# Moving the weight sums of a Strassen product behind its second product, and the setup's tables from GpSimd to VectorE

## The chip, the cores and the metric

The kernel runs on one core of a Trainium2 chip. The metric is the device time of one execution in microseconds, the median over the runs shown. Profiles come from one profiled execution; their times count from the start of its span.

## The reference

A decoder trunk of two layers on an input of 1024 tokens by 1024 features: an mLSTM layer (a matrix memory, worked through in chunks) and a layer of sliding-window attention with three dilations over a shared K and V. What matters here are the large projections around them, all in float32:

```python
# mLSTM layer, INNER_A = 2048, 4 heads of 512
xm, z, o_pre = jnp.split(x @ w_in, 3, axis=-1)
xc = jax.nn.silu(causal_dwconv(xm, conv_w, conv_b))
q = headwise(xc, wq)                       # blocks of 4 features, wq: 4x4 each
k = headwise(xc, wk)
v = headwise(xm, wv)
gates = jnp.concatenate([q, k, v], axis=-1) @ w_if + b_if
...
h = jax.nn.sigmoid(shp(o_pre).astype(jnp.float32)) * h_tilde
...
# shared K and V, once for three dilation groups
kv = (x @ w_kv).reshape(bsz, s, 2 * N_GROUPS_B, HEADS_B, HEAD_DIM_B)
```

The change touches the products for `o_pre` (weights in_w_o, two pairs of heads) and for the three V of the second layer (weights in_w_v, one per group), and the small tables made of wq, wk, wv and w_if at the start.

## The kernel before

A float32 product is made of three matmuls on split operands: `split` (L93, L94) casts a tile to a short float format on ScalarE (the high part, L93) and subtracts it from the tile on VectorE (the low part, L94); `mm3` (L98, L99, L100) multiplies high by high, high by low and low by high. So TensorE's L98 needs only L93, while L99 or L100 waits for L94.

The five large products with 512 columns run through `strassen_wide`. It is Strassen's scheme in Winograd's form: seven products of quarters in place of eight, with sums and differences of the weights' quarters (`sums`, L313, on VectorE, two instructions of 128x1024 for each sum) and of the results (`plus`, L317). A quarter of the weights is a pair of tiles that a DMA loads. The quarters are overwritten in place: b12 = b22 − b12, then b11 = b12 + b11, later b21 = b21 − b11 and b11 = b22 − b11. The products follow each other as b11, b21, then b11 (the new one), b12 and so on. Each `product` goes through four steps k; each step splits 128x512 of the weights into a pair of tiles (a ring of four slots in the w_o calls, s36, s37, s47, s49; of three in the w_v calls, s40, s41, s42) and issues four `mm3`, one for each of four PSUM banks.

`strassen_wide` is a generator; at each `yield` other work is put beside it: in the w_o calls the gate tables and the mLSTM's first steps, in the w_v calls the attention of the second layer. The order of each engine's instructions is not the order of the code: the program is scheduled by a simulated timeline (`schedule_with_timeline_sim=True`, L1678), which also lets `issue_after(instruction)` hold a block of instructions behind a given one. An engine runs its own list in that order, one after the other, and a wait for data holds up all that stands behind. The operands x of the second layer (the L144 and L154 differences of 128x1024 and their L93 and L94 splits) are made in the same time as the first w_v call, with the transposes L1022 and their evictions L1026 (VectorE) and L1028 (ScalarE) ahead of them.

`setup` makes the tables: `spread` (L419) puts the small blocks of wv on a 128x128 diagonal each, `through` (L426 to L428) multiplies w_if through wq, wk and wv, L457 adds two of the results, and a split makes `wprime`. The loads are in_wvT and in_wifr. All of that is on GpSimd (POOL). `setup_scores`, which the code puts in at the first `yield` of the second w_o call, uses the same two helpers. At the time of setup VectorE works for the first large product (the xm and z stream: L227, L233, L246, L250, L263, L264, L94).

Of the kernel before, what the change touches and what calls it, by code (L numbers as in the profile page):

```python
# [14 lines left out]
ALU = mybir.AluOpType  # L15
# [3 lines left out]
P = 128  # L19
# [4 lines left out]
NC_A = INNER // P  # L24
# [13 lines left out]
def f(ap):  # L38
    return ap.bitcast(F32)
# [22 lines left out]
class Kernel:  # L62
# [57 lines left out]
    def operands(self, raws, slots, engs, spare=None, s4_eng=None, fine=()):  # L120
# [3 lines left out]

        V, G = self.nc.vector, self.nc.gpsimd
        quarter = {"11": (0, 0), "12": (0, 1), "22": (1, 1), "s1": (0, 0), "s2": ("s2",) if spare else (1, 1), "s3": (1, 0), "s4": (0, 1)}
# [164 lines left out]
    def strassen_wide(self, raw, x, banks, dest, done, eng):  # L291


        V, A = self.nc.vector, self.nc.scalar
        sub, add = ALU.subtract, ALU.add
        b11, b12, b22, b21 = raw
        banks = Ring(*banks)
        new = lambda: [self.bank(i) for i in banks.next()]
        u2, u3 = [[t[:, j] for t in [self.slot(self.u_slots, (P, 2, 512)) for _ in range(2)] for j in range(2)]
                  for _ in range(2)]  # L300

        def product(acc, w, xp, first):
            for k in range(4):
                wh, wl = self.pair(self.w_hl)
                self.split(wh, wl, w[k // 2][:, k % 2 * 512:k % 2 * 512 + 512], eng)
                xh, xl = [p[k // 2][:, k % 2] for p in xp]
                for t in range(4):
                    ts = slice(t * P, t * P + P)
                    self.mm3(acc[t], xh[:, ts], xl[:, ts], wh, wl, first and k == 0, k == 3, skip=True)

        def sums(o, p, q, op):
            for j in range(2):
                eng.tensor_tensor(o[j], p[j], q[j], op=op)  # L313

        def plus(outs, ps, qs):
            for o, p, q in zip(outs, ps, qs):
                V.tensor_tensor(o, p, q, op=add)  # L317

        def result(half, i, p, q):
            o = dest(half, i)  # L320
            plus(o, p, q)
            done(half, i, o)

        a = new()
        product(a, b11, x["11"], True)
        yield
        for o, p in zip(u2, a):
            A.copy(o, p)
        sums(b12, b22, b12, sub)
        sums(b11, b12, b11, add)  # L330
        product(a, b21, x["12"], False)
        yield
        done(0, 0, a)
        b = new()
        product(b, b11, x["s2"], True)
        yield
        plus(u2, u2, b)
        c = new()
        product(c, b12, x["s3"], True)
        yield  # L340
        plus(u3, u2, c)
        sums(b21, b21, b11, sub)
        sums(b11, b22, b11, sub)
        d = new()
        product(d, b11, x["s1"], True)
        yield
        result(1, 1, u3, d)
        product(c, b21, x["22"], False)
        result(1, 0, u2, c)
        yield  # L350
        product(d, b22, x["s4"], False)
        result(0, 1, u2, d)
        yield
# [21 lines left out]
    def build(self):  # L375
        nc, tc = self.nc, self.tc
        with ExitStack() as top:
# [29 lines left out]
            self.dram["P"] = self.t(self.dp, [HA, SEQ], tag="dP")  # L407
            self.dram["G"] = self.t(self.dp, [HA, 64], tag="dG")
            self.attend = self.layer_a_attend()
# [4 lines left out]
            self.layer_b()  # L414


    def spread(self, dst, src, n):

        self.nc.gpsimd.tensor_tensor(dst.rearrange("p c (n j) -> p c n j", j=4),  # L419
                                     src.unsqueeze(2).to_broadcast([P, n, 32, 4]),  # L420
                                     self.mask.unsqueeze(1).unsqueeze(3).to_broadcast([P, n, 32, 4]), op=ALU.mult)

    def through(self, dst, w, rep, m):

        G = self.nc.gpsimd
        G.tensor_tensor(rep, rep, w.unsqueeze(3).to_broadcast([P, NC_A, 4, m]), op=ALU.mult)  # L426
        G.tensor_tensor(rep[:, :, 0:2], rep[:, :, 0:2], rep[:, :, 2:4], op=ALU.add)
        G.tensor_tensor(dst, rep[:, :, 0], rep[:, :, 1], op=ALU.add)  # L428

    def setup(self):  # L430


        nc, a, cp = self.nc, self.a, self.cp
        A, G = nc.scalar, nc.gpsimd
        self.mask = self.const("mask32", [P, 32], tag="em")
        w3 = self.slot(50, (P, 3, NC_A, 4))
        for i, n in enumerate("qkv"):
            nc.sync.dma_start(w3[:, i], a[f"w{n}T"])
        wqT, wkT, wvT = w3[:, 0], w3[:, 1], w3[:, 2]
        self.wv = []  # L440
        for i, c0 in enumerate((0, 7, 14)):
            n = (7, 7, 2)[i]
            t = self.slot(47 + i, (P, n, 136)) if i < 2 else self.t(cp, [P, n, 136], tag="k3")
            for c in range(n):
                self.wv.append(t[:, c])
            self.spread(t[:, :, 0:P], wvT[:, c0:c0 + n], n)
        g3 = self.t(cp, [P, 3, NC_A, 8], tag="k2")
        gates = []
        for i, w in enumerate((wqT, wkT, wvT)):
            rep = self.slot(51, (P, NC_A, 4, 8))  # L450
            nc.sync.dma_start(rep, a["wifr"][i])
            g = g3[:, i]
            self.through(g, w, rep, 8)
            gates.append(g)
        for c in range(NC_A):
            A.copy(self.wv[c][:, P:P + 8], gates[2][:, c])
        G.tensor_tensor(gates[0], gates[0], gates[1], op=ALU.add)  # L457
        self.wprime = self.t(cp, [P, NC_A, 16], F32R, tag="k1")
        self.split(self.wprime[:, :, 0:8], self.wprime[:, :, 8:16], gates[0], G)

    def setup_scores(self):
        nc, a = self.nc, self.a
        t = self.slot(40)
        w, wkr, at = [t[:, lo:hi] for lo, hi in ((0, 64), (64, 320), (320, 384))]
        w, at = [v.rearrange("p (c i) -> p c i", i=4) for v in (w, at)]
        wkr = wkr.rearrange("p (c i m) -> p c i m", i=4, m=4)
        nc.sync.dma_start(w, a["wqT"])
        nc.sync.dma_start(wkr, a["wkr"])
        self.through(at, w, wkr, 4)
        for i in range(2):  # L470
            bd = self.slot(41 + i, (P, 8, P))
            self.spread(bd, at[:, 8 * i:8 * i + 8], 8)
            for j in range(2):
                cs = slice(512 * j, 512 * j + 512)
                hl = self.slot(43 + j, (P, 2, 512), F32R)
                self.split(hl[:, 0], hl[:, 1], bd.rearrange("p c m -> p (c m)")[:, cs], nc.gpsimd)
                nc.sync.dma_start(self.dram["A", i][:, :, cs], f(hl))
# [1204 lines left out]
```

## Time and profile before

| | |
|---|---|
| median of 3 runs | 2017.71 us (2016.01 to 2018.58) |
| the profiled execution | 2017.29 us, of which the span is 2015.5 us |
| mean granted clock | 0.996 |
| TensorE busy | 97% of the span |
| VectorE, ScalarE, GpSimd busy | 72%, 49%, 8% |

A row of the timeline gives the start in the span, the duration, the engine, the line, what is written and read (buffer numbers left out), the shape, and in brackets how long the engine had been idle before and what ended it. A duration on VectorE overlaps a little with that of its neighbour, so that the distance of two starts is what an instruction costs in a row of many. TensorE's matmuls of 128x512 follow each other at 0.23 us though each is shown with 0.39.

### The profile page before, as it was taken

To read this page: it belongs to the slowest core of one execution; us is meant where nothing else is said; L and a number is where in the kernel's file an instruction comes from. 1 tells how busy PE (TensorE), PEld (TensorE's weight loads), DVE (VectorE), ACT (ScalarE), POOL (GpSimd) and SP (SyncE) were. 2 spreads that over 40 slices of the span, in tenths; PEclk is the share of its full clock that TensorE was granted. 3 is DMA by queue.
4 is the path that set the end of the run, shared out by engine and by line. 5 is a ranking of instruction groups with operands and counts; after the bars stand their busy time and mean duration, and the time that the engine had idled before them with its cause. 6 is when DMAs were issued, how large, how long until landed. Compare 5 with 4: busy or idle time off the path is not lost.

```text
span 2015.5 us, 26595 instructions
## 1 busy us (share of the span) xinstructions
PE 1962.4 (97%) x9521; PEld 1626.3 (81%) x9521; DVE 1444.8 (72%) x2854; ACT 992.5 (49%) x1990; POOL 158.7 (8%) x127
## 2 busy tenths in 40 slices
PE   9999999999999999999999999999999999999997
PEld 7778888778888888878788888877887788887776
DVE  8778778675577776457867765776568887776878
ACT  5455555535645543343524542565255456676621
POOL 0200000022145343000000000000000000000000
PEclk9999999999999999999999999999999999999999
DMA  4445464456754543526121143225325622224753
GB/s 170 146 164 193 164 224 172 147 172 227 271 204 164 192 163 117 184 62 232 53 73 53 55 154 106 71 97 178 134 91 203 225 95 85 84 95 154 269 198 126
DMA packets 117916, 300.65 MB, mean 149 GB/s; under 512 B 13652, under 2 KB 31508, under 8 KB 117784
## 3 DMA queue, kind: packets, MB, share of 16 engines
q1 hardware_dynamic: 117784, 298.95, 43.2%
q8 instruction: 75, 1.23, 0.3%
q14 instruction: 57, 0.47, 0.1%
HBM read 206.32 MB, written 92.59 MB: 148 GB/s over the span
## 4 chain that ended last, share of the span: by engine, by line
PE 73%; DVE 12%; DMA 8%; ACT 4%; issue 2%; SPq 0%; POOL 0%; DVEq 0%; ACTq 0%
PE b L98 23%; PE b L100 22%; PE b L99 22%; DVE s L94 3%; DMA s<-in_w_qk 2%; PE b L603 1%; DMA s<-df 1%; ACT s L93 1%; PE b L1278 1%; DMA s<-in_w_z 1%; ACT s L1264 1%; DMA s<-in_xq 1%; PE b L609 1%; PE b L878 1%; DVE s L1415 1%
## 5 line engine op out<-in xcount | busy, mean ns | idle before, releaser
L99 PE MATMUL b<-s,s 128*128 128x512 f32 (+3 forms) x2720 | 1035.3, 382 | 9.2 <-DVE s L94 9.2
L100 PE MATMUL b<-s,s 128*128 128x512 f32 (+3 forms) x2720 | 1021.3, 382 | 4.8 <-DVE s L94 4.7
L98 PE MATMUL b<-s,s 128*128 128x512 f32 (+2 forms) x2720 | 1001.2, 386 | 20.1 <-ACT s L93 16.3
L94 DVE TENSOR_TENSOR s<-s,s 128x512 fp32r<-128x512 f32 (+2 forms) x704 | 507.5, 736 | 279.1 <-ACT s L93 273.4
L93 ACT CAST s<-s 128x512 fp32r<-128x512 f32 (+2 forms) x708 | 436.6, 636 | 541.2 <-PE b L100 308.8
L98 PEld LDWEIGHTS b<-s,s 128*128 128x128 f32 x2720 | 511.7, 188 | 124.7 <-ACT s L93 24.4
L99 PEld LDWEIGHTS b<-s,s 128*128 128x128 f32 x2720 | 512.4, 188 | 107.3 <-DVE s L94 13.2
L100 PEld LDWEIGHTS b<-s,s 128*128 128x128 f32 x2720 | 510.5, 188 | 105.5 <-DVE s L94 9.5
L233 DVE TENSOR_TENSOR s<-s,b 128x512 f32<-128x512 f32 x132 | 89.8, 681 | 27.3 <-PE b L100 25.9
L1264 ACT ACTIVATE s<-s,nmax 128x128 f32<-128x128 f32 (+1 forms) x192 | 84.3, 441 | 45.9 <-DVE nmax L1262 45.6
L94 DVE TENSOR_TENSOR s<-b,s 128x512 fp32r<-128x512 f32 (+1 forms) x96 | 51.5, 552 | 34.7 <-ACT s L93 34.3
L568 DVE SCALAR_TENSOR_TENSOR s<-s,c_convw,s 128x512 f32<-128x512 f32 (+3 forms) x96 | 71.5, 755 | 3.1 <-ACT s L565 2.6
L227 DVE TENSOR_TENSOR s<-s,b 128x512 f32<-128x512 f32 x88 | 59.5, 679 | 16.2 <-PE b L100 11.5
L317 DVE TENSOR_TENSOR s<-s,b 128x512 f32<-128x512 f32 x100 | 63.3, 680 | 8.1 <-PE b L100 7.8
L246 DVE TENSOR_TENSOR s<-s,s 128x512 f32<-128x512 f32 x44 | 30.3, 690 | 50.5 <-DMA s<-in_w_qk 23.5
L812 ACT ACTIVATE s<-s,k 128x128 f32<-128x128 f32 x144 | 47.2, 392 | 39.0 <-DVE s L94 18.5
L313 DVE TENSOR_TENSOR s<-s,s 128x1024 f32<-128x1024 f32 x40 | 49.6, 1247 | 20.8 <-DMA s<-in_w_o 11.7
L1260 DVE CUSTOM_DVE_ANT_0 s<-b,k 128x128 f32<-128x128 f32 (+1 forms) x192 | 57.2, 345 | 6.5 <-PE b L100 4.4
L93 ACT CAST s<-b 128x512 fp32r<-128x512 f32 (+1 forms) x96 | 43.8, 479 | 23.4 <-PE b L100 13.4
L771 POOL TENSOR_TENSOR s<-s 128x512 fp32r<-128x512 f32 x32 | 43.5, 1372 | 75.2 <-ACT s L770 65.5
L1211 DVE SCALAR_TENSOR_TENSOR s<-s,s 128x512 fp32r<-128x512 f32 x48 | 42.4, 885 | 9.6 <-ACT s L1210 9.1
L882 POOL TENSOR_TENSOR s<-s,s 128x512 f32<-128x512 f32 x32 | 42.3, 1337 | 65.0 <-DVE s L881 48.5
(182 smaller groups left out, 1489.0 us busy)
## 6 DMA issues: line engine op xcount, KB each, us to landing
s<-in_w_qk SPq DMA_DIRECT2D x48, 512.0 KB
s<-in_w_out SPq DMA_DIRECT2D x40, 512.0 KB
dp<-s SPq DMA_DIRECT2D x32, 512.0 KB
s<-dp SPq DMA_DIRECT2D x32, 512.0 KB
s<-in_w_v SPq DMA_DIRECT2D x24, 512.0 KB
dg<-s SPq DMA_DIRECT2D x24, 512.0 KB
s<-dg SPq DMA_DIRECT2D x24, 512.0 KB
s<-df SPq DMA_DIRECT2D x24, 512.0 KB
```

The costliest lines, as they stand in the source:

```text
L93: self.nc.scalar.copy(h, src)
L94: self.last_split = (l_eng or self.nc.vector).tensor_tensor(l, src, f(h), op=ALU.subtract)
L98: mm(ps, lh, rh, start=start, stop=False, skip_group_check=skip)
L99: mm(ps, lh, rl, start=False, stop=False, skip_group_check=skip)
L100: mm(ps, ll, rh, start=False, stop=stop, skip_group_check=skip)
L227: V.tensor_tensor(o, p, q, op=add)
L233: V.tensor_tensor(o, p[lane][rows], q[lane][rows], op=add)
L313: eng.tensor_tensor(o[j], p[j], q[j], op=op)
L317: V.tensor_tensor(o, p, q, op=add)
L568: V.scalar_tensor_tensor(u[i][:, lo:o + 512], xm[i][:, lo - s:o + 512 - s], convw[:, c, 3 - s:4 - s], u[i][:, lo:o + 512], op0=ALU.mult, o ...
L1260: V.tensor_tensor_reduce(out=dst, in0=sc, in1=bias, op0=ALU.add, op1=ALU.max, scale=1.0, scalar=-3e38, accum_out=mx[:, b:b + 1])
L1264: self.last_exp = A.activation(res[b][0], res[b][0], AF.Exp, bias=nm[:, b:b + 1], accum_out=stat[:, 1, g, b:b + 1])
```

## The change

In `strassen_wide` the sums b12 and b11 are issued after the low part of the last split of the second product. In `setup`, `spread`, `through`, the sum of gates and the low part of `wprime` are on VectorE; `setup_scores` hands in GpSimd, as before.

```diff
@@ strassen_wide
         for o, p in zip(u2, a):
             A.copy(o, p)
-        sums(b12, b22, b12, sub)
-        sums(b11, b12, b11, add)
         product(a, b21, x["12"], False)
+        with self.tc.issue_after(self.last_split.ins):
+            sums(b12, b22, b12, sub)
+            sums(b11, b12, b11, add)
         yield
@@ spread, through, setup
-    def spread(self, dst, src, n):
-        self.nc.gpsimd.tensor_tensor(...)
+    def spread(self, dst, src, n, eng):
+        eng.tensor_tensor(...)
-    def through(self, dst, w, rep, m):
-        G = self.nc.gpsimd
-        G.tensor_tensor(rep, rep, w.unsqueeze(3).to_broadcast([P, NC_A, 4, m]), op=ALU.mult)
-        G.tensor_tensor(rep[:, :, 0:2], rep[:, :, 0:2], rep[:, :, 2:4], op=ALU.add)
-        G.tensor_tensor(dst, rep[:, :, 0], rep[:, :, 1], op=ALU.add)
+    def through(self, dst, w, rep, m, eng):
+        eng.tensor_tensor(rep, rep, w.unsqueeze(3).to_broadcast([P, NC_A, 4, m]), op=ALU.mult)
+        eng.tensor_tensor(rep[:, :, 0:2], rep[:, :, 0:2], rep[:, :, 2:4], op=ALU.add)
+        eng.tensor_tensor(dst, rep[:, :, 0], rep[:, :, 1], op=ALU.add)
-            self.spread(t[:, :, 0:P], wvT[:, c0:c0 + n], n)
+            self.spread(t[:, :, 0:P], wvT[:, c0:c0 + n], n, V)
-            self.through(g, w, rep, 8)
+            self.through(g, w, rep, 8, V)
-        G.tensor_tensor(gates[0], gates[0], gates[1], op=ALU.add)
+        V.tensor_tensor(gates[0], gates[0], gates[1], op=ALU.add)
-        self.split(self.wprime[:, :, 0:8], self.wprime[:, :, 8:16], gates[0], G)
+        self.split(self.wprime[:, :, 0:8], self.wprime[:, :, 8:16], gates[0])
@@ setup_scores
-        self.through(at, w, wkr, 4)
+        self.through(at, w, wkr, 4, nc.gpsimd)
-            self.spread(bd, at[:, 8 * i:8 * i + 8], 8)
+            self.spread(bd, at[:, 8 * i:8 * i + 8], 8, nc.gpsimd)
```

Since the timeline orders the program anew, other rows move with these. Below, names carry the tile's number; a number that differs by a few between the two programs is the same tile of the text.

VectorE in the second w_o pair, before. The splits s36_648 to s47_651 are the weights of the first pair's last product (quarter b22, tiles s32_589 and s33_590); s52_661 is half of the second pair's b12.

```order
L94 TENSOR_TENSOR s36_648_3670<-s32_589_3195,s36_648_3670 128x512
L313 TENSOR_TENSOR s52_661_3774<-s35_663_3778,s52_661_3774 128x1024
L94 TENSOR_TENSOR s37_649_3685<-s32_589_3195,s37_649_3685 128x512
L317 TENSOR_TENSOR s38_646_3658<-s8_591_3199,b4_624_3450 128x512
L94 TENSOR_TENSOR s49_650_3700<-s33_590_3196,s49_650_3700 128x512
```

The same place in the changed program, and then the place where the sum stands now, behind s47_686, the last split of product 2.

```order
L94 TENSOR_TENSOR s36_648_3670<-s32_589_3195,s36_648_3670 128x512
L94 TENSOR_TENSOR s37_649_3685<-s32_589_3195,s37_649_3685 128x512
L317 TENSOR_TENSOR s38_646_3658<-s8_591_3199,b4_624_3450 128x512
L94 TENSOR_TENSOR s49_650_3700<-s33_590_3196,s49_650_3700 128x512
L317 TENSOR_TENSOR s38_646_3658<-s8_591_3199,b5_625_3451 128x512
```

```order
L94 TENSOR_TENSOR s47_686_3924<-s33_659_3770,s47_686_3924 128x512
L313 TENSOR_TENSOR s48_660_3773<-s34_662_3777,s48_660_3773 128x1024
L313 TENSOR_TENSOR s52_661_3774<-s35_663_3778,s52_661_3774 128x1024
L313 TENSOR_TENSOR s50_656_3765<-s48_660_3773,s50_656_3765 128x1024
L313 TENSOR_TENSOR s51_657_3766<-s52_661_3774,s51_657_3766 128x1024
L313 TENSOR_TENSOR s32_658_3769<-s32_658_3769,s50_656_3765 128x1024
L94 TENSOR_TENSOR s36_693_3955<-s50_656_3765,s36_693_3955 128x512
```

The split s37_649 has no sum in front of it any more; the first split of product 3, s36_693, has five.

VectorE in the first w_v call, before: s41_1505 is the last split of product 2, s42_1512 the first of product 3 (weights b11 in s44 and s45). L154, L246 and the 128x1024 L94 are other work.

```order
L94 TENSOR_TENSOR s41_1505_8608<-s52_1455_8386,s41_1505_8608 128x512
L154 TENSOR_TENSOR s31_1493_8537<-s37_1481_8498,s35_1478_8487 128x1024
L94 TENSOR_TENSOR s3_1539_8848<-s37_1481_8498,s2_1538_8847 128x1024
L246 TENSOR_TENSOR s38_1564_9011<-s39_1565_9013,s38_1564_9011 128x512
L94 TENSOR_TENSOR s17_1529_8776<-s14_1356_7791,s16_1528_8775 128x1024
L94 TENSOR_TENSOR s42_1512_8633<-s44_1452_8381,s42_1512_8633 128x512
```

The same stretch in the changed program, from s41_1505 on, in two pieces that follow each other.

```order
L94 TENSOR_TENSOR s41_1505_8604<-s52_1455_8386,s41_1505_8604 128x512
L313 TENSOR_TENSOR s28_1456_8389<-s50_1458_8393,s28_1456_8389 128x1024
L313 TENSOR_TENSOR s29_1457_8390<-s51_1459_8394,s29_1457_8390 128x1024
L144 TENSOR_TENSOR s15_1362_7817<-s31_1493_8537,s15_1362_7817 128x1024
L144 TENSOR_TENSOR s33_1365_7830<-s33_1365_7830,s31_1493_8537 128x1024
L94 TENSOR_TENSOR s21_1495_8540<-s30_1492_8535,s20_1494_8539 128x1024
```

```order
L94 TENSOR_TENSOR s23_1497_8544<-s31_1493_8537,s22_1496_8543 128x1024
L94 TENSOR_TENSOR s17_1529_8776<-s14_1356_7791,s16_1528_8775 128x1024
L246 TENSOR_TENSOR s38_1564_9011<-s39_1565_9013,s38_1564_9011 128x512
L313 TENSOR_TENSOR s44_1452_8381<-s28_1456_8389,s44_1452_8381 128x1024
L313 TENSOR_TENSOR s45_1453_8382<-s29_1457_8390,s45_1453_8382 128x1024
L94 TENSOR_TENSOR s37_1587_9197<-s34_1506_8623,s36_1586_9196 128x256
L94 TENSOR_TENSOR s19_1531_8780<-s15_1362_7817,s18_1530_8779 128x1024
L94 TENSOR_TENSOR s37_1587_9197<-s35_1507_8624,s36_1586_9196 128x256
L94 TENSOR_TENSOR s31_1543_8858<-s33_1365_7830,s30_1542_8857 128x1024
L313 TENSOR_TENSOR s46_1454_8385<-s46_1454_8385,s44_1452_8381 128x1024
L94 TENSOR_TENSOR s42_1512_8633<-s44_1452_8381,s42_1512_8633 128x512
```

Between the two splits stand fifteen rows where four stood: five sums (b12 in s28 and s29, b11 in s44 and s45, half of b21 in s46), and operand rows that came behind s42_1512 before. L154 s31 and L94 s3 stand ahead of s41_1505 now, L94 s21 behind it.

VectorE in setup, in the changed program: s36_276 and s8_278 are low parts that TensorE's next two products wait for. Before, the rows L94, L250, L263, L94 stood there one behind the other, and the L419 to L428 rows (L420 here) on GpSimd.

```order
L420 TENSOR_TENSOR s47_257_864<-s50_256_860,em_255_858 128x7x128
L420 TENSOR_TENSOR s48_258_866<-s50_256_860,em_255_858 128x7x128
L420 TENSOR_TENSOR k3_259_868<-s50_256_860,em_255_858 128x2x128
L94 TENSOR_TENSOR s36_276_919<-s32_269_910,s36_276_919 128x512
L426 TENSOR_TENSOR s51_261_871<-s51_261_871,s50_256_860 128x512
L250 TENSOR_TENSOR s32_269_910<-s32_269_910 128x512
L427 TENSOR_TENSOR s51_261_871<-s51_261_871 128x16x16
L263 TENSOR_TENSOR s33_270_912<-s33_270_912,s32_269_910 128x512
L428 TENSOR_TENSOR k2_260_870<-s51_261_871 128x128
L94 TENSOR_TENSOR s8_278_952<-s32_269_910,s8_278_952 128x512
```

The three spreads stand ahead of the first of the two splits, and the first `through` between the two.

More of the change, by code (lines that the diff above doesn't have):

```diff
@@ L414, in build @@
             self.layer_b()
-    def spread(self, dst, src, n):
-        self.nc.gpsimd.tensor_tensor(dst.rearrange("p c (n j) -> p c n j", j=4),
+    def spread(self, dst, src, n, eng):
+        eng.tensor_tensor(dst.rearrange("p c (n j) -> p c n j", j=4),
                                      src.unsqueeze(2).to_broadcast([P, n, 32, 4]),
                                      self.mask.unsqueeze(1).unsqueeze(3).to_broadcast([P, n, 32, 4]), op=ALU.mult)
-    def through(self, dst, w, rep, m):
-        G = self.nc.gpsimd
-        G.tensor_tensor(rep, rep, w.unsqueeze(3).to_broadcast([P, NC_A, 4, m]), op=ALU.mult)
-        G.tensor_tensor(rep[:, :, 0:2], rep[:, :, 0:2], rep[:, :, 2:4], op=ALU.add)
-        G.tensor_tensor(dst, rep[:, :, 0], rep[:, :, 1], op=ALU.add)
+    def through(self, dst, w, rep, m, eng):
+        eng.tensor_tensor(rep, rep, w.unsqueeze(3).to_broadcast([P, NC_A, 4, m]), op=ALU.mult)
+        eng.tensor_tensor(rep[:, :, 0:2], rep[:, :, 0:2], rep[:, :, 2:4], op=ALU.add)
+        eng.tensor_tensor(dst, rep[:, :, 0], rep[:, :, 1], op=ALU.add)
     def setup(self):
         nc, a, cp = self.nc, self.a, self.cp
-        A, G = nc.scalar, nc.gpsimd
+        A, V = nc.scalar, nc.vector
         self.mask = self.const("mask32", [P, 32], tag="em")
```

## The prediction

> **What bounds the kernel.** I read the page first (busy shares, then the chain that ended last), then each of the five places where the wide products run, and setup: TensorE's and VectorE's timelines there, and windows for busy shares and clock.
>
> ```profile
> span 2015.5 us, 26595 instructions
> PE 1962.4 (97%) x9521; PEld 1626.3 (81%) x9521; DVE 1444.8 (72%) x2854; ACT 992.5 (49%) x1990; POOL 158.7 (8%) x127
> PE 73%; DVE 12%; DMA 8%; ACT 4%; issue 2%; SPq 0%; POOL 0%; DVEq 0%; ACTq 0%
> ...
> L313 DVE TENSOR_TENSOR s<-s,s 128x1024 f32<-128x1024 f32 x40 | 49.6, 1247 | 20.8 <-DMA s<-in_w_o 11.7 <-DMA s<-in_w_v 8.6
> ```
>
> TensorE works 97% of the span, 53 us are left, and the change takes no matmul away. So it can only close or open TensorE's waits, or shift its clock. L313 is the moved code: 40 sums in five calls, four of the eight in each call moved. 20.8 us of VectorE's idle time stands in front of L313, all of it for loads. That matters where TensorE waits for something queued behind the sum.
>
> **Second w_o pair: a stall that goes.** VectorE (three rows), TensorE (one), then windows whose columns are busy time of PE, PEld, DVE, ACT, POOL, the granted clock, DMA share and GB/s.
>
> ```profile
> 443.42 1.23 DVE L313 TENSOR_TENSOR s<-s,s 128x1024 f32<-128x1024 f32 x1 [5.19 <-DMA s<-in_w_o]
> 444.56 0.69 DVE L94 TENSOR_TENSOR s<-s,s 128x512 fp32r<-128x512 f32 x1
> 445.17 0.68 DVE L317 TENSOR_TENSOR s<-s,b 128x512 f32<-128x512 f32 x1
> ...
> 445.31 0.80 PE L99 MATMUL b<-s,s 128*128 128x512 f32 x1 [2.61 <-DVE s L94]
> ...
> 441.39:444.80 3.41, 1.30 (x6) 0.75 (x4) 1.38 (x2) 0.00 (x0) 0.00 (x0) 1.00 0.14 49
> 444.80:448.21 3.41, 2.90 (x7) 2.35 (x8) 3.41 (x7) 2.25 (x4) 0.00 (x0) 0.50 0.44 150
> ```
>
> A sum waits 5.19 us for its load with the split L94 (s37_649) of the previous pair's last product behind it; TensorE waits 2.61 us for that split and then gets half clock for one window of 3.41 us. In that window TensorE was busy 2.90 us, half of which full clock would have saved: 1.45 us. The changed order puts the sums behind the new pair's product 2, so both go: −2.61 − 1.45 = −4.1 us. The loads of b21 gain too, since the freed slot is the one that split reads. At the new place the sums stand ahead of the split for product 3; there I find room of about a microsecond, against GpSimd work that slows VectorE beside it: +0.2 (0 to +0.5).
>
> The Trainium skill, "TensorE: Matmul & The Clock Gate", Part 1 "The HAM clock gate", says that the clock halves after an idle window of 4096 cycles, 3413 ns, in windows that run free of the kernel. The trace agrees on the length; here the window before had 1.30 us of work and was not idle throughout, so the measured row decides.
>
> **First w_v call: a stall that grows.** VectorE's timeline, the window around it, and TensorE's.
>
> ```profile
> 948.14 3.62 DVE L313 TENSOR_TENSOR s<-s,s 128x1024 f32<-128x1024 f32 x3 [1.84 <-DMA s<-in_w_v]
> 972.60 1.23 DVE L313 TENSOR_TENSOR s<-s,s 128x1024 f32<-128x1024 f32 x1
> 976.50 1.23 DVE L313 TENSOR_TENSOR s<-s,s 128x1024 f32<-128x1024 f32 x1
> 983.45 1.22 DVE L144 TENSOR_TENSOR s<-s,s 128x1024 f32<-128x1024 f32 x1
> 997.47 2.42 DVE L94 TENSOR_TENSOR s<-s,s 128x1024 fp32r<-128x1024 f32 x3
> 999.81 1.22 DVE L313 TENSOR_TENSOR s<-s,s 128x1024 f32<-128x1024 f32 x1
> 1000.94 2.35 DVE L144 TENSOR_TENSOR s<-s,s 128x1024 f32<-128x1024 f32 x2
> 1003.21 2.49 DVE L94 TENSOR_TENSOR s<-s,s 128x1024 fp32r<-128x1024 f32 x4
> 1005.62 1.22 DVE L313 TENSOR_TENSOR s<-s,s 128x1024 f32<-128x1024 f32 x1
> ...
> 984.00:999.00 15.00, 12.11 (x53) 9.28 (x51) 15.00 (x16) 11.92 (x19) 0.00 (x0) 1.00 0.12 36
> ...
> 994.74 0.50 PE L99 MATMUL b<-s,s 128*128 128x512 f32 x1 [0.73 <-DVE s L94]
> 996.46 0.39 PE L100 MATMUL b<-s,s 128*128 128x512 f32 x1
> 999.35 0.50 PE L99 MATMUL b<-s,s 128*128 128x512 f32 x1 [2.50 <-DVE s L94]
> ```
>
> Those five (three at 948.14, one at 972.60, one at 976.50) lie in slack. From 983.45 VectorE has no idle time: it makes layer B's x operands, and is busy 15.00 of the 15.00 us that the window shows. TensorE already waits for it, 2.50 us at 999.35, for the split s42_1512 that opens product 3 (the last of the 128x1024 and 512 rows at 997.47). In the changed order five sums (the moved four, and b21 − b11, which needs them) stand in this saturated stretch ahead of s42_1512, and five more instructions of 128x1024 with them (L144 s15 and s33, L94 s23, s19 and s31), and the two small L94 s37 of 128x256, all of which were behind it. One 128x1024 costs 1000.94 − 999.81 = 1.13 us back to back; the four at 1003.21 give way to the next L313 at 1005.62, so one of 1024, one of 512 and the two small ones take 2.41; a 512 takes 0.61 (445.17 − 444.56), which leaves 0.67 for the two. So 10 × 1.13 + 0.67 = 12.0 us. Without the sums VectorE starts the stretch up to 0.4 us earlier: it is bound there by TensorE's transposes. Net +11.6; I take +11.5, bounds 10.5 (an extra microsecond of earlier start) and 12.5 (a wait of VectorE for one of ScalarE's casts, which stand between, of about 1 us). Nothing hides it: the end of s42_1512 moves from about 999.3 to 1010.8, and TensorE has nothing else in its queue.
>
> TensorE then stands still from about 997 to 1010.8 but for a few matmuls. By the rows at 441.39 and 444.80, a window with 1.30 of 3.41 us busy is followed by one at half clock. From the resumption the rest of the running window is at half (half of up to 3.41 us lost), and the next too if this one was mostly idle. That is +1.5 us at the measured price of 1.45, between 0.7 and 2.4 by the phase.
>
> **Second and third w_v calls, first w_o pair.**
>
> ```profile
> 1194.74 1.37 DVE L94 TENSOR_TENSOR s<-s,s 128x512 fp32r<-128x512 f32 x2 [1.36 <-ACT s L93]
> 1200.91 0.39 PE L99 MATMUL b<-s,s 128*128 128x512 f32 x1
> ...
> 1389.75 1.23 DVE L313 TENSOR_TENSOR s<-s,s 128x1024 f32<-128x1024 f32 x1 [2.43 <-DMA s<-in_w_v]
> 1398.44 1.37 DVE L94 TENSOR_TENSOR s<-s,s 128x512 fp32r<-128x512 f32 x2 [1.12 <-ACT s L93]
> 1394.51 0.50 PE L99 MATMUL b<-s,s 128*128 128x512 f32 x1 [0.80 <-DVE s L94]
> 1404.62 0.39 PE L99 MATMUL b<-s,s 128*128 128x512 f32 x1
> ...
> 387.28 1.23 DVE L313 TENSOR_TENSOR s<-s,s 128x1024 f32<-128x1024 f32 x1
> 396.91 0.39 PE L99 MATMUL b<-s,s 128*128 128x512 f32 x1
> ```
>
> Second call: product 2's last split is the first of the two at 1194.74, the second is product 3's first, s42_1770. Five sums now come between: 1195.4 + 5 × 1.13 + 0.69 = 1201.8, and TensorE wants it at 1200.91: +0.85 (0 to +1.5). Third call: the sum that waits 2.43 us for its load no longer stands ahead of product 2's split, so the 0.80 us wait goes; the same five sums between the two splits at 1398.44 put the second at 1399.1 + 5.65 + 0.69 = 1405.4, 0.8 behind the need at 1404.62. Net 0.0 (−0.8 to +0.8). First w_o pair: the five sums and two gate rows of some 0.7 come between product 2's last split, after which the L313 at 387.28 started, and product 3's: 387.3 + 5.65 + 1.4 + 0.69 = 395.0, ahead of the L99 that reads it at 396.91, so it is covered. The score tables of GpSimd then come some 9 us later, beside VectorE's work of 425 to 430: +0.3 (0 to +1.5).
>
> **Setup: the tables on VectorE.** VectorE, GpSimd, TensorE, and the waits of TensorE between 85 and 130 us.
>
> ```profile
> 88.80 0.69 DVE L94 TENSOR_TENSOR s<-s,s 128x512 fp32r<-128x512 f32 x1 [0.61 <-ACT s L93]
> 89.53 2.07 DVE L250 TENSOR_TENSOR s<-s 128x512 f32<-128x512 f32 x1
> 93.62 1.10 DVE L94 TENSOR_TENSOR s<-s,s 128x512 fp32r<-128x512 f32 x1
> ...
> 89.34 3.81 POOL L419 TENSOR_TENSOR s<-s,em 128x896 f32<-128x896 f32 x2 [88.89 <-DMA s<-in_wvT]
> 104.90 1.09 POOL L426 TENSOR_TENSOR s<-s,s 128x512 f32<-128x512 f32 x1 [2.26 <-DMA s<-in_wifr]
> ...
> 94.78 0.50 PE L100 MATMUL b<-s,s 128*128 128x512 f32 x1 [1.74 <-DVE s L94]
> ...
> PE b L98 <- ACT s L93: 1.1, 3, 0.6
> ```
>
> VectorE takes over two spreads of 128x896 (896/1024 × 1.13 = 0.99 each), one of 256 (0.34), three sets of 512, 256 and 128 elements (about 0.61 + 0.34 + 0.2) and two small ones: 6.1 to 6.7 us. In return VectorE is rid of a neighbour: L250 took 2.07 us beside GpSimd's L419, and the split at 93.62 took 1.10 where the one at 88.80 took 0.69. In the changed order three spreads, which cannot start before their load at 89.34, stand ahead of the split of 88.80, which so ends at 89.34 + 2.3 + 0.7 = 92.3 instead of 89.5; TensorE's next product waits for it. The following split (93.62, done 94.72) is then due at about 95.4, because L426, L427, L428 stand between but L250 and L263 are back at 0.6. So TensorE, which had waited 1.74 us there anyway, loses 0.7 more. The third L426 waits for its load on VectorE now; behind it VectorE is about 1 us ahead, so part of the 1.1 us of ScalarE waits goes. If the new idle stretch halves a clock window, up to 1.5 more. Net +0.8 (−0.4 to +2.5).
>
> The Trainium skill, "SBUF — State Buffer", "SBUF: two separate sides", says that VectorE with two SBUF inputs and GpSimd share a port pair as an exclusive lock, the loser blocked for the whole instruction. L250 at 2.07 us agrees. By that rule alone this part would gain what rival B below gives.
>
> **Sum.** Setup +0.8, first pair +0.3, second pair −4.1 + 0.2, w_v +11.5 + 1.5, +0.85, 0.0: +11.1 us. The profiled execution took 2017.29 us (span 2015.5 and 1.8 around it), 0.4 below the median of 2017.71; 2017.3 + 11.1 = 2028.4.
>
> **Rivals.** A: the sums cost nothing at the first w_v call (its waits stay as they are), and only the gains stand: −3.9 − 0.8 + 0.8 + 0.3 = 2013.7, faster. It decides there: if the work put ahead of s42_1512 ended by about 999.3, the change would win. Against it stands the 15.00 of 15.00; for it only that part of the moved operand work could find idle time before 983.45, where the transposes still hold the operands back. B: freeing GpSimd's port gives more than the tables cost in setup: the 1.74 and the 1.1 us of waits go, −2.8 instead of +0.8, in all 2024.8; for it speaks L250's 2.07, against it the three spreads in front of the split. C: the clock is halved over two windows after each of the long stalls, and the w_v stretch takes 12.5: +1.0 + 1.7 + 1.5 in setup, 2032.6. D: gains and losses cancel, within 0.2% (some 4 us, about what a measurement of this kernel can tell from no change): that needs the w_v stall at 4 instead of 13 us, which only a much shorter queue ahead of s42_1512 would give.
>
> **How the numbers follow.** The forecast as summed 0.50, B 0.16, C 0.20, A 0.06, D 0.08. Predicted 2028.4. The range leaves out A and D: 2022.0 below (B, with the w_v stall at 10.5, the clock at 0.7 and the second call at 0, gives 2022.2) to 2033.5 above (C with 0.9 for first pair and second call). Faster 0.06, same 0.08, slower 0.86.
>
> **What the profile would show.** At 445 no wait of 2.6 us and no window at 0.50. Around 997 to 1011 two idle stretches of TensorE, of some 8 and 4 us, before L99 of product 3, with L313 five times in VectorE's gapless stretch, and a half-clock window behind. At 1201 a wait below 1 us. At 89.5 a wait of nearly 3 us, and L250 near 0.6. I am wrong if VectorE turns out to have slack in that stretch, or if its waits there are for ScalarE instead.

## The result and the profile after

The changed kernel took 2028.76 us (median of 7 runs, 2024.85 to 2032.31), the kernel before 2018.04 us beside it (7 runs): a ratio of 1.0052, 95% interval 1.0037 to 1.0067. It is slower by 10.7 us, where 11.1 were forecast.

The profiled execution is the fastest of the seven, 2024.85 us. From its page: the span and busy rows, the chain, and the group of the moved sums.

```profile
span 2023.0 us, 26593 instructions
PE 1968.1 (97%) x9521; PEld 1631.8 (81%) x9521; DVE 1443.5 (71%) x2868; ACT 994.6 (49%) x1990; POOL 142.2 (7%) x113
...
PE 78%; DVE 10%; DMA 7%; ACT 2%; issue 2%; SPq 0%; DVEq 0%; ACTq 0%
...
L313 DVE TENSOR_TENSOR s<-s,s 128x1024 f32<-128x1024 f32 x40 | 48.5, 1244 | 0.1
```

The sums do what the change says: VectorE's idle time in front of L313 went from 20.8 to 0.1 us. No engine has more work, but TensorE is busy 5.7 us longer with the same 9521 matmuls, as more of them ran at half clock. Not all of that is the change: a second profile of the kernel before (e5) shows 1966.1 us, 3.7 more than the first. The longest stretch at half clock, 20.5 us from 992.4 on, is at the first w_v call. First the timeline there, TensorE's rows and then VectorE's.

```profile
993.18 0.79 PE L99 MATMUL b<-s,s 128*128 128x512 f32 x1 [2.87 <-DVE s L94]
1003.51 2.07 PE L98 MATMUL b<-s,s 128*128 128x512 f32 x4 [6.55 <-ACT s L93]
1008.68 0.79 PE L99 MATMUL b<-s,s 128*128 128x512 f32 x1 [3.09 <-DVE s L94]
1009.27 0.63 PE L100 MATMUL b<-s,s 128*128 128x512 f32 x1
...
993.04 2.35 DVE L313 TENSOR_TENSOR s<-s,s 128x1024 f32<-128x1024 f32 x2
995.31 2.35 DVE L144 TENSOR_TENSOR s<-s,s 128x1024 f32<-128x1024 f32 x2
997.59 3.49 DVE L94 TENSOR_TENSOR s<-s,s 128x1024 fp32r<-128x1024 f32 x3
1001.59 2.35 DVE L313 TENSOR_TENSOR s<-s,s 128x1024 f32<-128x1024 f32 x2
1003.86 3.02 DVE L94 TENSOR_TENSOR s<-s,s 128x256 fp32r<-128x256 f32 x4
1006.80 1.22 DVE L313 TENSOR_TENSOR s<-s,s 128x1024 f32<-128x1024 f32 x1
1007.94 0.68 DVE L94 TENSOR_TENSOR s<-s,s 128x512 fp32r<-128x512 f32 x1
```

The window around it (its length, busy time of PE, PEld, DVE, ACT and POOL with their instructions, granted clock, DMA share, GB/s):

```profile
984.00:1011.00 27.00, 14.48 (x46) 10.36 (x45) 27.00 (x29) 11.71 (x17) 0.00 (x0) 0.66 0.06 19
```

VectorE is busy 27.00 of 27.00 us. The five sums stand in that queue, and s42_1512, the split at 1007.94, ends at 1008.6. TensorE stands still 2.87 + 6.55 + 3.09 us, with a few matmuls between, and goes on at a pitch of 0.43 us (1009.27, next at 1009.70) where full clock gives 0.23. The first wait, for product 2's last split, the prediction did not name; it is the same queue and does not move its end. The second is shown as one for ScalarE's cast, but that cast waits for a sum, the first half of b11 (VectorE's L313 at 1001.59):

```profile
1002.84 1.76 ACT L93 CAST s<-s 128x512 fp32r<-128x512 f32 x3 [2.96 <-DVE s L313]
```

How the places add up is read best from one and the same matmul in two traces: both programs issue 9521, so the n-th matmul's start, minus its start in the first profile of before, says how late TensorE is there. Worked out so from the traces, in us, with before's time, rounded, at the head of a column (the kernels are those of the next part; the extra matmuls of e8 aren't counted):

| kernel | 88 | 93 | 133 | 442 | 450 | 744 | 993 | 1002 | 1197 | 1202 | 1392 | 1398 | 1413 | 2004 |
|---|---|---|---|---|---|---|---|---|---|---|---|---|---|---|
| after | 0.0 | +5.3 | +1.2 | +1.5 | −2.7 | −1.9 | −2.8 | +11.3 | +10.9 | +11.9 | +12.4 | +11.3 | +12.3 | +7.7 |
| e5 before again | 0.0 | +0.8 | +0.9 | +0.9 | −1.3 | +0.2 | +0.1 | +1.0 | +1.4 | +1.4 | +2.2 | +2.5 | +2.5 | +2.8 |
| e1 sums only | +0.4 | +1.6 | +1.6 | +1.8 | −2.5 | −1.8 | −2.8 | +11.6 | +11.6 | +12.6 | +12.2 | +11.1 | +12.1 | +11.8 |
| e2 tables only | +0.1 | +4.8 | +0.5 | +1.0 | −1.5 | −0.3 | −0.9 | −1.2 | −1.2 | −1.2 | +2.1 | +2.4 | +2.4 | +2.8 |
| e3 not first w_v | +1.6 | +2.8 | +3.4 | +3.3 | −0.9 | +2.9 | +3.1 | +3.1 | +3.1 | +4.1 | +4.4 | +3.3 | +4.2 | +2.7 |
| e4 w_o only | 0.0 | +0.9 | +1.4 | +1.4 | −2.8 | −0.9 | −0.6 | +0.8 | +0.5 | +0.5 | +0.1 | +0.4 | +0.4 | +2.5 |
| e6 halves | +0.5 | +5.8 | +1.7 | +2.9 | −1.4 | +2.0 | +1.8 | +13.8 | +13.9 | +13.9 | +13.5 | +12.4 | +12.4 | +11.8 |
| e7 operands behind | −0.2 | +4.0 | +0.3 | +0.7 | −3.6 | −1.9 | −3.0 | +3.4 | +3.7 | +4.7 | +4.6 | +3.5 | +4.5 | +4.1 |
| e8 filled | 0.0 | +3.8 | −0.4 | −0.1 | −4.4 | −3.2 | −3.2 | +9.0 | +8.6 | +9.6 | +11.8 | +10.7 | +11.7 | +9.1 |
| e9 best | +0.4 | +1.0 | +1.0 | +2.4 | −1.9 | +1.1 | +2.1 | −1.7 | −1.1 | −1.1 | +1.0 | −0.1 | −0.1 | −1.8 |
| e10 operands, early sums | 0.0 | +0.5 | +1.3 | +1.7 | −0.6 | +2.3 | +3.0 | −0.8 | +1.2 | +1.2 | +3.2 | +3.5 | +3.5 | +3.9 |
| e11 best, free slots | +0.2 | −0.8 | −0.8 | −0.4 | −4.7 | −0.5 | −1.0 | −4.9 | −2.8 | −2.8 | −0.2 | −1.3 | −1.3 | −2.9 |
| e12 w_o, free slots | 0.0 | −0.2 | −0.5 | +0.1 | −4.1 | +0.7 | +1.2 | +1.2 | +1.2 | +1.2 | +2.9 | +3.3 | +3.3 | +6.8 |

A step between two neighbouring columns is what a place costs. Row e5 is the same program as the first profile: steps of 1 to 2 us between executions are no effect of an edit. What counts are steps that all kernels with an edit share and none without it has.

### The profile page after: what moved, and what is told of

Same layout as the page of the kernel before. It is cut to its first block, busy times and chain, and to the rows that moved or that the text cites. A ratio compares the mean times of both kernels' runs of the same rounds, so it can differ in the third digit from the quotient of the medians.

```text
span 2023.0 us, 26593 instructions
## 1 busy us (share of the span) xinstructions
PE 1968.1 (97%) x9521; PEld 1631.8 (81%) x9521; DVE 1443.5 (71%) x2868; ACT 994.6 (49%) x1990; POOL 142.2 (7%) x113
## 4 chain that ended last, share of the span: by engine, by line
PE 78%; DVE 10%; DMA 7%; ACT 2%; issue 2%; SPq 0%; DVEq 0%; ACTq 0%
PE b L98 24%; PE b L100 24%; PE b L99 24%; DVE s L94 3%; DMA s<-df 2%; PE b L603 1%; DMA s<-in_w_qk 1%; PE b L1278 1%; PE b L609 1%; ACT s L93 1%; DMA ds<-s 1%; DMA df<-s 1%; DMA s<-in_xq 1%; PE b L878 1%; DVE s L1417 1%
## 5 line engine op out<-in xcount | busy, mean ns | idle before, releaser
L94 DVE TENSOR_TENSOR s<-s,s 128x512 fp32r<-128x512 f32 (+2 forms) x704 | 507.3, 736 | 307.0 <-ACT s L93 301.7
L99 PEld LDWEIGHTS b<-s,s 128*128 128x128 f32 x2720 | 513.7, 189 | 107.2 <-DVE s L94 12.4
L94 DVE TENSOR_TENSOR s<-b,s 128x512 fp32r<-128x512 f32 (+1 forms) x96 | 51.4, 552 | 36.2 <-ACT s L93 36.0
L246 DVE TENSOR_TENSOR s<-s,s 128x512 f32<-128x512 f32 x44 | 30.3, 690 | 41.8 <-DMA s<-in_w_qk 21.0
L313 DVE TENSOR_TENSOR s<-s,s 128x1024 f32<-128x1024 f32 x40 | 48.5, 1244 | 0.1
```

The costliest lines, as they stand in the source:

```text
L94: self.last_split = (l_eng or self.nc.vector).tensor_tensor(l, src, f(h), op=ALU.subtract)
L99: mm(ps, lh, rl, start=False, stop=False, skip_group_check=skip)
```

## The experiments

Ratios are to the kernel before, run beside on the same chip.

**e1 to e4: the parts apart.** e1 is the changed kernel with setup's tables back on GpSimd. e2 has the tables on VectorE and the sums early. In e3 and e4 the tables are on GpSimd and `strassen_wide` takes a flag:

```diff
-        product(a, b21, x["12"], False)
-        with self.tc.issue_after(self.last_split.ins):
-            sums(b12, b22, b12, sub)
-            sums(b11, b12, b11, add)
+        if not late:
+            sums(b12, b22, b12, sub)
+            sums(b11, b12, b11, add)
+        product(a, b21, x["12"], False)
+        if late:
+            with self.tc.issue_after(self.last_split.ins):
+                sums(b12, b22, b12, sub)
+                sums(b11, b12, b11, add)
```

with `late` True in the w_o calls of both, and in the w_v calls `g > 0` (e3) or False (e4).

> All five calls issue the sums late, the tables stay on GpSimd. Theory (the late sums cost at the first w_v call and gain at the second w_o pair, the tables cost 1.7 us in setup): before -4.1 +13.2 +0.75 -0.25 = about 2027.6 us; in the profile no wait at 445, TensorE idle some 12 us before product 3 of the first w_v call. Rival (the sums cost nothing there by themselves, the loss comes with the tables and the order that they give): about 2014.

Measured: 2029.09 us, ratio 1.0062 (1.0048 to 1.0077). The sums alone make the whole loss, and the step at 993 to 1002 is 14.4 us (after: 14.1). The rival is out.

> The sums stand where they stood before, the tables of setup are on VectorE. Theory: TensorE about 1.7 us later from 130 us on and nothing after that, 2019.7 us, with the wait of 2.7 us for the split behind the spreads and a half-clock window after it. Rival (free of GpSimd's neighbourhood VectorE gains more than it takes over): 2.8 us less than before, 2015.2.

Measured: 2018.5 us, ratio 1.0001 (0.9988 to 1.0014). Neither figure came. TensorE is 4.8 us late at 93, as in the changed kernel, and 0.5 at 133; the kernel before, profiled again, has 0.9 there. So the tables' delay is made up within 40 us. How, the part on the prediction says.

> Sums late in both w_o pairs and in the second and third w_v call, early in the first; tables on GpSimd. Theory: -4.1 (second pair) +0.75 (second w_v call) -0.25 (third) = 2014.4 us, and no long wait near 1000 beyond the 0.7 and 2.5 us of before. Rival (late sums cost wherever VectorE has operand work or attention beside them, so in the other w_v calls too): 2018 or more.

Measured: 2017.95 us, ratio 0.9998 (0.9988 to 1.0008). With the first w_v call spared the loss is gone, so the other calls cost little: in the table 1.0 us at the second call (1197 to 1202), and −1.1 and +0.9 at the third. But the gain of 3.6 us didn't come either: a miss of the theory's sum.

> Sums late in the two w_o pairs alone, tables on GpSimd. Theory: -4.1 us, 2013.9 us, the second w_o pair without its 2.6 us wait and without the half-clock window, the w_v calls as before. Rival (the wait comes back as another, at product 3 of that pair or at a later load): 2016 to 2018.

Measured: 2017.26 us, ratio 0.9989 (0.9976 to 1.0002): some 2 us less, if anything, where 4 were expected.

**e5: how much of the 4 us is one execution's.**

> The kernel before, profiled once more, to see how much one execution's places differ from another's. Expected if the +1.4 to +3.4 us that four profiles showed at 200 us (with either engine for the tables) and the 1.7 to 4.3 us that the second w_o pair gave are differences of executions: setup again later than in the first profile by 1 us or more, and a wait at 445 between 0.5 and 2.6 us. If they belong to the edits: both as in the first profile within 0.3 us.

VectorE's timeline at the sum, and then TensorE's waits between 430 and 455 us (in total, times, longest), in this second profile of before:

```profile
443.47 1.23 DVE L313 TENSOR_TENSOR s<-s,s 128x1024 f32<-128x1024 f32 x1 [4.41 <-DMA s<-in_w_o]
```

```profile
PE b L99 <- DVE s L94: 1.8, 1, 1.8
```

Setup is 0.9 us late again (column 133), a little under the 1 us expected, and the wait is within its range: both are mostly differences of executions. The load lands at 443.47 as it did at 443.42 (443.23 in e2, 444.16 in e10), but TensorE came 0.9 us later to it. Its wait is 1.8 instead of 2.6 us, and no half-clock window follows. From 442 to 450 all ten kernels with late sums there gain 4.2 to 4.3 us against the first profile; of those with early sums e5 gains 2.1, e10 2.3 and e2 2.5. So the late sums gain 1.7 to 2.1 us over these three, 4.2 over the first. Where the sums are early, the wait for the load also takes up what is late before it, up to its own length; where they are late, there is no wait and a delay stays.

The rest of e3's gap: its timeline, TensorE and ScalarE.

```profile
467.39 0.50 PE L98 MATMUL b<-s,s 128*128 128x512 f32 x1 [1.25 <-ACT s L328]
...
465.19 1.14 ACT L93 CAST s<-s 128x512 fp32r<-128x512 f32 x2 [3.78 <-DMA dA<-s]
```

ScalarE's cast of a score table waits for the store of the table before it, which holds the slot; behind it stand the evictions L328 that free product 1's banks. This wait was covered while TensorE stood still for the load. Now it shows in four of the eight kernels that have late sums and these slots: 1.25 us (e3), 0.80 (e4), 0.73 (e9), 0.51 (e6); not in the changed kernel's own profile.

**e6: two sums fewer in the queue.** `product` gets a hook after its second split, and the sums go by halves:

```diff
         with self.tc.issue_after(self.last_split.ins):
-            sums(b12, b22, b12, sub)
-            sums(b11, b12, b11, add)
+            eng.tensor_tensor(b12[0], b22[0], b12[0], op=sub)
+            eng.tensor_tensor(b11[0], b12[0], b11[0], op=add)
...
+                if k == 2 and behind:    # in product 3
+                    with self.tc.issue_after(self.last_split.ins):
+                        behind()         # the same two for [1]
```

> As the changed kernel, but only the first halves of b12 and b11 are issued behind product 2's last split; the second halves behind the second split of product 3. So three sums instead of five stand ahead of product 3's first split. Theory (the end of VectorE's queue sets it): 2 x 1.13 = 2.3 us less at the first w_v call, and the waits of the second and third w_v call (0.75 and 0.7 us) gone: 2028.8 - 3.7 = 2025. Rival (what delays that split is the operand rows and the clock, not the sums): 2028 to 2029.

Measured: 2030.2 us, ratio 1.0044 (1.0029 to 1.0059), which can't tell 2025 from 2028 us. The trace can: the step at the first w_v call is 12.0 us (changed kernel 14.1), the one at 1202 is gone (0.0 against +1.0), and the one at 1413 too. Of TensorE's waits from 985 to 1016 us these are left:

```profile
PE b L98 <- ACT s L93: 7.1, 1, 7.1
PE b L99 <- DVE s L94: 4.8, 2, 2.8
```

The sums' share is as the theory has it (2.1 for 2.3), within what the clock's phase leaves open.

**e7: the other rows of that queue.**

```diff
             for n, _ in enumerate(steps):
+                if g == 0 and n == 0:
+                    with self.tc.issue_after(self.last_split.ins):
+                        x["s1"], x["s4"]
                 if g == 0 and n == 2:
-                    x["22"], x["s4"]
+                    x["22"]
```

> As the changed kernel, but the operands x s1 and s4 of the first w_v call (four L144 and three L94 of 128x1024 among those ahead of product 3's first split) are issued behind the last split of product 3. The sums stay late. Theory: 7 x 1.13 = 7.9 us less in the queue, the first split of product 3 ends that much earlier, 2028.8 - 7.9 = 2021, or 2020 with a shorter time at half clock. Rival (ScalarE's casts or TensorE's transposes hold that split): no more than 2 us less.

Measured: 2023.72 us, ratio 1.0015 (1.0004 to 1.0026), 7.5 us less than the changed kernel's 1.0052 by the ratios. The step is 6.4 instead of 14.1 us, 7.7 less for seven instructions of 1.13. TensorE's waits from 985 to 1012:

```profile
PE b L98 <- ACT s L93: 4.8, 1, 4.8
PE b L99 <- DVE s L94: 1.4, 2, 0.8
```

So sums and operands cost there alike: each instruction of 128x1024 ahead of the split is 1.0 to 1.1 us of TensorE.

**e8: the clock's share.** After product 2's last matmul 40 matmuls with operands at hand go into product 3's banks:

```diff
+        if fill:
+            xh, xl = [p[0][:, 0] for p in x["12"]]
+            with self.tc.issue_after(self.last_mm.ins):
+                for k in range(fill):
+                    self.nc.tensor.matmul(b[k % 4], xh[:, 0:P], xl, start=True, stop=True, skip_group_check=True)
         product(b, b11, x["s2"], True)
```

> As the changed kernel, with 40 extra matmuls of 128x512 into the banks of product 3 before its first matmul overwrites them, in the time in which TensorE stands still at the first w_v call. They take about 10 us of an idle 12. Theory (product 3 begins at half clock because TensorE stood still, about 2 us): the first L99 of product 3 comes at the same time, what follows runs at full clock, 2026.8. Rival (the slow matmuls after the wait have another cause, or the extra work only delays): 2028.8 or more.

Measured: 2026.37 us, ratio 1.0034 (1.002 to 1.0047), an interval that overlaps the changed kernel's. Its timeline (TensorE) and its window, as shown of the changed kernel:

```profile
992.76 0.50 PE L99 MATMUL b<-s,s 128*128 128x512 f32 x1 [2.82 <-DVE s L94]
995.65 9.91 PE L340 MATMUL b<-s,s 128*128 128x512 f32 x40
1008.25 0.50 PE L99 MATMUL b<-s,s 128*128 128x512 f32 x1 [1.78 <-DVE s L94]
1008.60 0.40 PE L100 MATMUL b<-s,s 128*128 128x512 f32 x1
1008.84 0.40 PE L99 MATMUL b<-s,s 128*128 128x512 f32 x1
```

```profile
984.00:1011.00 27.00, 22.40 (x91) 17.69 (x90) 27.00 (x29) 11.99 (x18) 0.00 (x0) 0.94 0.06 20
```

The split still ends at 1008.2, but what follows runs at 0.24 us a matmul. The step is 12.2 us instead of 14.1: the half clock costs 1.9 us of it. In the trace, work without a use made this place faster. The Trainium skill, "TensorE: Matmul & The Clock Gate", Part 1 "The HAM clock gate", has the clock come back after about one busy window of 3.4 us; the trace agrees: from 993.62 to 997.03 TensorE is busy all 3.41 us at a granted clock of 0.51, and the two windows behind are at 1.00.

**e9 to e12: a version that beats both.** e9 puts together what gained: sums late by halves in the w_o calls and in the third w_v call, early in the first two, e7's edit, tables on GpSimd. e10 is the kernel before with e7's edit alone.

> What the runs point to: sums late, by halves, in the w_o pairs and in the third w_v call; early in the first two w_v calls; the operands x s1 and s4 of the first w_v call behind product 3's last split; tables on GpSimd. Theory: 2 to 4 us at the second w_o pair (the wait for its load differs from one execution to the next), 3.2 us at the first w_v call (both waits of before), 1 us at the third: 6 to 8 us less than before, a ratio of 0.996 to 0.997. Rival (TensorE gives it back at later loads or at the layer's end): a ratio of 0.999 to 1.000.

Measured: 2016.8 us, ratio 0.9984 (0.997 to 0.9997): faster than before, by some 3 us where 6 to 8 were expected.

> The kernel before with one edit alone: the operands x s1 and s4 of the first w_v call behind product 3's last split; sums early everywhere, tables on GpSimd. Theory: the waits of 0.7 and 2.5 us at the first w_v call go, 3.2 us less, a ratio of 0.998 to 0.999, and 1.4 to 2.6 us of wait at the second w_o pair stay. Rival (the operands are wanted so early that product 5 waits for them): a ratio of 1.000 or more.

Measured: 2019.64 us, ratio 0.9992 (0.998 to 1.0005), not told from no change. The waits at 995 and 999 are gone, but TensorE waits 1.5 us shortly behind, in two pieces, for later splits, which now stand behind the held rows; of the 3.8 us gained from 993 to 1002, 1.8 are left at 1197:

```profile
PE b L99 <- DVE s L94: 1.5, 2, 1.2
```

e11 is e9, and e12 is e4, with the score tables' slots freed, so that the cast of the e3 rows need not wait for the store:

```diff
-                hl = self.slot(43 + j, (P, 2, 512), F32R)
+                hl = self.slot(43 + 2 * i + j, (P, 2, 512), F32R)
```

> As the kernel of e9, and the four score tables go through four slots (43 to 46) instead of two used twice, so that ScalarE's cast of the second pair of them doesn't wait for the store of the first. Theory (at the second w_o pair the time won came back in part as ScalarE's wait for that store, 0.5 to 1.25 us of TensorE's at product 2's end): no wait for the store there, up to 1 us less than e9, a ratio of 0.9975 to 0.998. Rival (the wait moves on to the next thing late, the loads of dv at 473): as e9, 0.9984.

Measured: 2014.21 us, ratio 0.9962 (0.9948 to 0.9975), the fastest of all. From 441 to 448 and from 984 to 1012 TensorE has next to no idle time and full clock:

```profile
441.39:448.21 6.82, 6.82 (x31) 5.63 (x30) 4.50 (x8) 4.50 (x8) 0.00 (x0) 1.00 0.77 267
984.00:1012.00 28.00, 27.75 (x122) 22.21 (x121) 28.00 (x32) 18.13 (x27) 0.00 (x0) 1.00 0.07 20
```

and no wait of 0.2 us or more between 446 and 536. Behind 1012 the two pieces of e10 are here too (1.5 us), and of the 3.9 us gained from 993 to 1002, 1.8 are left at 1197. That it beats e9 by 0.2%, some 4 us, is more than the store's wait explains, and the two intervals overlap; how much of it is the slots stays open.

> As the kernel of e4 (sums late in the w_o pairs alone) with the same four slots for the score tables. Theory: the wait of 0.8 us at the end of product 2 of the second pair is gone, a ratio of 0.998 to 0.9985. Rival: another wait takes its place, 0.9989 as e4.

Measured: 2019.83 us, ratio 0.9993 (0.9983 to 1.0004): the rival by the trace, while the interval just reaches the theory's ratio. The wait for the store is gone, but 0.41 us remain at 463 for another load (dv), and 0.96 us at product 3's first split is new:

```profile
476.40 0.50 PE L99 MATMUL b<-s,s 128*128 128x512 f32 x1 [0.96 <-DVE s L94]
```

In front of it stand the five sums, which took 7.95 us here, with GpSimd at work beside them for 4.35 of the 8.00 us from 466.70; in the changed kernel's profile the five took 5.76 us and no such wait is there. With the halves (e11) it isn't there either.

## Why the prediction was right, and where its terms were off

**First w_v call: right.** Forecast +11.5 and +1.5 for the clock, 13.0; measured 14.1 in one profile and 14.4 in another (e1), of which 1.9 are clock (e8), so that the queue's share is some 12.2. Queue and end of the split came as worked out (forecast 1010.8, 2.8 early by the second pair's gain: 1008.0; seen 1008.6). e6 and e7 bear out the price of each row.

**Second w_o pair: right in kind, too large.** Forecast −3.9 net. Against the profile it was worked out from, −4.3. But that profile had the longest wait of the four of before's order (2.6 us; the others 1.8, 1.4 and, in e10, 1.6) and was the only one with a half-clock window. The size that counts for a median is about 2 us. The term that was mis-sized is this one, −4.1: it takes one execution's wait and half-clock window, at a load that lands within 1 us of the same time in four profiles while TensorE comes to it up to 1.7 us later, for the kernel's. The wait at product 3 that I set at 0.2 is not in the changed kernel's profile; the wait for the score table's store, 0.5 to 1.3 us, I had not seen.

**Setup: right mechanism, its size not told from nothing.** Forecast +0.8. The rows of the changed kernel, VectorE and TensorE:

```profile
90.02 2.09 DVE L420 TENSOR_TENSOR s<-s,em 128x896 f32<-128x896 f32 x2 [1.00 <-DMA s<-in_wvT]
92.37 0.68 DVE L94 TENSOR_TENSOR s<-s,s 128x512 fp32r<-128x512 f32 x1
94.12 0.69 DVE L250 TENSOR_TENSOR s<-s 128x512 f32<-128x512 f32 x1
...
93.11 0.80 PE L100 MATMUL b<-s,s 128*128 128x512 f32 x1 [2.72 <-DVE s L94]
94.12 0.63 PE L99 MATMUL b<-s,s 128*128 128x512 f32 x1
```

The wait of nearly 3 us is there (2.72), the half clock that I gave a chance is there (0.43 us a matmul), L250 is back at 0.69, and TensorE is 5.3 us late at 93. The forecast is net of waits that the kernel before has behind that: 1.8 us are made up at before's wait of 1.74 at 94.78, which leaves 3.5, more than the forecast's upper end of 2.5, and another 1.7 around its waits for ScalarE's casts of 122 and 124 us. At 133 it is 1.2 late (e2 0.5). But the kernel before, profiled again, is 0.9 late there and doesn't have those last waits either, and e1, with the tables on GpSimd, is 1.6 late. Over all traces the five kernels with the tables on VectorE lie at −0.4 to +1.7 there and the eight other profiles of the table at −0.8 to +3.4. So the delay is real at 93, and at 133 it is lost among the executions; e2 has the term at 0 within 0.14%. Rival B, a gain there, didn't come.

**Second and third w_v calls: right.** Forecast +0.85 and −0.8 + 0.8; the steps are +1.0 and −1.1 + 1.0 in the changed kernel and in e1, and within 0.1 of that in e3. **First w_o pair:** forecast +0.3, nothing seen (from 380 to 400 us the changed kernel's step is 0.0).

The sum of 11.1 came out at 10.7, closer than its terms were, and that closeness is luck: with the w_v stall 1.1 to 1.4 larger, setup 0.8 smaller and the second pair's gain some 2 smaller it would be about 13. The interval (0.37 to 0.67% of 2018 us, 7.5 to 13.5) holds both, and so does that of e1. The two profiled executions are 7.6 us apart; the changed kernel's made up 2.6 us between 1857 and 1906 us, counted as in the table, where the other profiles lie between −1.4 and +0.6. What sets that is open.

## What to carry to other kernels

Before work is put behind something on an in-order engine, read the engine's busy share in the stretch where it will stand, not over the span: the sums were moved out of a wait for a load at one call and into a queue without a gap at another, and that one call cost several times what the other gained. A wait that ends when a load lands hides what is late ahead of it, up to its length; taking it away shows the next thing late (here a store that holds a slot), and its price from one profile is one execution's. Where two instructions must stand in front of a critical split, put only the halves that the split needs there.

## What the runs showed of the hardware

TensorE's clock halves though the window was not idle: 1.30 of 3.41 us busy ahead of the half window at 444.80 in the kernel before. In each trace the stretches at half clock start and end on a grid of 3.413 us, within 0.004 us from 20 to 2000 us, and the grid lies elsewhere in each execution. So the same wait of 2.50 us at 999 falls differently in two executions of one program, first the kernel before, then e5 (windows as above):

```profile
997.77:1001.18 3.41, 1.83 (x8) 1.54 (x9) 3.41 (x5) 1.85 (x5) 0.00 (x0) 1.00 0.00 0
1001.18:1004.59 3.41, 3.41 (x17) 2.83 (x16) 3.41 (x4) 2.39 (x3) 0.00 (x0) 1.00 0.00 0
...
997.58:1001.00 3.42, 1.57 (x7) 1.31 (x8) 3.42 (x5) 2.13 (x6) 0.00 (x0) 0.99 0.00 0
1001.00:1004.41 3.41, 3.41 (x10) 2.64 (x9) 3.41 (x4) 2.13 (x3) 0.00 (x0) 0.51 0.00 0
```

With 1.83 us of matmuls in the window the next is at full clock, with 1.57 at half. Counted so over the 14 traces, all 50 full-clock windows with less than 1.59 us of work were followed by half clock, 11 of the 95 with 1.59 to 2.3, and none with more. What a wait costs in clock can therefore not be told from its length alone; the 1.45 us at the second w_o pair came in one of four executions.

Matmuls that nobody needs, put into the wait, saved 1.9 us of the step there. And the same program's executions lie as far apart as 2016.3 to 2028.3 us (23 runs in one comparison), so that an edit of 2 us was told from none only in the traces.
